# A DRAIN on GpSimd's queue behind its last adding transfer, in a hybrid Mamba-2 and latent-attention layer

## The chip, the cores and the metric

The kernel runs on one core of a Trainium2 chip. Five engines work side by side, each with its own queue of instructions: TensorE (PE) multiplies matrices, VectorE (DVE) and ScalarE (ACT) do elementwise work, GpSimd (POOL) does elementwise work and issues transfers, and SyncE (SP) only issues transfers and waits. They are kept in step by semaphores. A DRAIN is an instruction on such a queue that does no work: what stands behind it waits until the DRAIN is done. The metric is the device time of one execution in microseconds (us). The kernel before takes 643.44 us, the median of 3 runs (643.41 to 643.98).

## The reference, cut to what matters

The program computes one layer of a streaming encoder for 512 prompt tokens and 64 tokens of a running stream, together 576 columns of a transposed activation: a normalisation, a projection, a state-space branch and a latent-attention branch, an output projection, a gated feed-forward block, and a last normalisation.

```python
def hybrid_layer(x, ckv_past, krope_past, ssm_h0, conv_buf, p):
    h = rmsnorm(x, p['norm_mix'])
    proj = h @ p['w_in']
    ...
    x = x + jnp.concatenate([y_ssd, o], axis=-1) @ p['w_out']
    hf = rmsnorm(x, p['norm_ffn'])
    x = x + (jax.nn.silu(hf @ p['w_gate']) * (hf @ p['w_up'])) @ p['w_down']
    return x, c_kv, k_rope, h_new, conv_new

y_prompt = rmsnorm(xp, norm_final)
y_sample = rmsnorm(xs, norm_final)
```

What bears on this change is the end: the last part of the product with `w_down`, added to `x`, and the last `rmsnorm` over 1024 channels.

## The kernel before, in words

Activations lie with channels on the 128 partitions and the 576 tokens along the free axis, so 1024 channels are 8 tiles, numbered `t`. Each fp32 operand is split into a high and a low part, and a product is three matrix multiplications.

The feed-forward block runs over 22 tiles of `d_ff` in parts (`CUTS`). While TensorE computes gate and up for one part, it also computes `w_down` for the part before. These partial sums don't stay on the chip's memory near the engines: `acc[0]` and `acc[1]` are two arrays in DRAM. The first part is written there (`down_plain`, lines 1009 and 1012), the four next parts are added by transfers that GpSimd issues with `accum_op=ALU.add` (`send`, line 1064). After the last of them each half of `acc[0]` (four tiles) is read back by SP (line 1143) into the tile `sum_0` or `sum_1`, and the same half of `acc[1]` is added onto it by two transfers of GpSimd (line 1145), four in all. These are GpSimd's last adding transfers, and the last transfers that it issues at all.

Then comes the last part of the product (`NL` tiles of `d_ff`, weights `wd`), done for two groups of tokens, `parts`: columns 0 to 319 and 320 to 575. For each group and tile TensorE multiplies (line 988), VectorE adds the result to `sum` (line 1163), ScalarE squares it (line 1202 in the first group, 1251 in the second) and scales it (line 1167). The squares are summed over tiles in `ss3`, which lies in the tile `fz`. In the first group GpSimd adds tiles 0, 2 and 4 (line 1207, three TENSOR_TENSOR), VectorE sums the others in `sq_last` and adds them at the end (lines 1212 and 1210). TensorE sums `ss3` over channels (line 1244), and ScalarE and VectorE turn that into the factor of the normalisation. In the second group GpSimd adds seven tiles (line 1256). The outputs are multiplied by the factor on VectorE (lines 1177 and 1173), two of the second group on GpSimd (line 1175, the last two TENSOR_TENSOR), and sent out by SP and ScalarE (line 1183).

Behind this the framework puts the end of the program, which the profile shows at line 1482, where the program is finished: SP waits for every outstanding transfer; every engine runs a DRAIN; PE, DVE, ACT and SP report to a semaphore; GpSimd, after its own DRAIN, waits for the four reports and releases the four. Semaphores are then cleared and the same exchange is done once more. The start of the program (line 1479) has one such exchange too.

The order of each engine's instructions is written out by hand: the table `ISSUE` holds, for each engine, the places of its instructions in the order of their making, and `issue_in_order` ties each to the next. GpSimd's row ends with

```python
137 136 138 140 139 141-143 145 144 146-148
```

Places 144 to 148 are transfers of line 1064. The four of line 1145 (149 to 152) and the twelve TENSOR_TENSOR (153 to 164) are not in the row; they keep the order in which they are made.

Of the kernel before, what the change touches and what calls it, by code (L numbers as in the profile page):

```python
# [54 lines left out]
def hybrid_layer_kernel(ctx: ExitStack, tc: tile.TileContext, a, o):  # L55
    nc = tc.nc
    pe, act, dve, pool, sp = nc.tensor, nc.scalar, nc.vector, nc.gpsimd, nc.sync
# [1082 lines left out]
    for i2, tag in enumerate(("bc", "sz")):  # L1140
        x2t[i2] = z = midp.tile([P, 4, T], F32, tag=tag, name=f"sum_{i2}")
        rows = lambda i, n: acc[i][n].rearrange("t p c -> p t c")
        sp.dma_start(z, rows(0, slice(4 * i2, 4 * i2 + 4)))
        for j in (0, 2):
            pool.dma_start(z[:, j : j + 2], rows(1, slice(4 * i2 + j, 4 * i2 + j + 2)), accum_op=ALU.add)
        x2.extend(z[:, j] for j in range(4))

    NL = len(prev)
    wd = [weights(a["w_dlast"][i], 1024, f"dl{i}") for i in range(NL)]
# [236 lines left out]
    "POOL": """  # L1386
0-3 7 18 28 4 8 5 9 6 10 26 11 27 12 29 13-17 20-23 19 24-25 31 30 32-42 53 55 57 59 54 56 58 60 43-52 61-69 71 73 75
70 77 79 81 74 76 72 83 78 80 82 84-87 89 88 90 92 91 93-103 105 104 106 108 107 109-119 121 120 122 124 123 125-135
137 136 138 140 139 141-143 145 144 146-148
""",  # L1390
    "SP": """
11-14 16 15 17-20 23 22 25 21 24 31 26 32 39-40 36 33 38 41-42 37 43-47 55 77 62 79 54 56 58 63 81 57 60 59 61 68 66
# [102 lines left out]
```

## Time and profile before

| what | value |
|---|---|
| median of 3 runs (lowest to highest) | 643.44 us (643.41 to 643.98) |
| the profiled execution, its own time | 643.93 us |
| its span, first to last instruction | 642.2 us |
| granted TensorE clock, mean | 0.995 |
| busy: PE, DVE, ACT, POOL | 626.6, 543.0, 400.7, 110.2 us |

Each time in a view counts from the start of the span. A row of the timeline gives start, duration, engine, line, operation, the tile written and the tile read, and in brackets how long the engine had been idle and what ended that. DRAINs and semaphore instructions run on an engine's queue (POOLq, SPq and so on) and aren't counted as busy time, so they are missing from the busy rows and are seen in the view of their line.

### The profile page before, as it was taken

What the parts mean: (1) busy time and instruction counts of PE and PEld (TensorE: products, weight loads), DVE (VectorE), ACT (ScalarE), POOL (GpSimd) and SP (SyncE); (2) the same over time, 40 slices, a digit from 0 to 9 for tenths busy, and PEclk for the clock granted to TensorE, in tenths of its full rate; (3) what the DMA queues carried; (4) which work ended last, traced back from release to release, by engine and by line L of the source; (5) the groups of instructions that cost most, each with busy time, mean ns of one, the idle gap of its engine ahead of it and who ended that gap; (6) DMA issues with size and microseconds to landing.
All of it is one profiled execution on the core that took longest, in us unless ns stands there. A gap on an engine that the chain in (4) does not pass through costs nothing.

```text
span 642.2 us, 12089 instructions
## 1 busy us (share of the span) xinstructions
PE 626.6 (98%) x4635; PEld 598.8 (93%) x4635; DVE 543.0 (85%) x945; ACT 400.7 (62%) x768; POOL 110.2 (17%) x164
## 2 busy tenths in 40 slices
PE   9998999999999999999999999999999999999994
PEld 8898999986788799999999999999999999999993
DVE  6998986899876699999999879988898889976554
ACT  7644436678775567766556666566657665765463
POOL 1321103101010000001301330033103210332323
PEclk9999999999999999999999999999999999999998
DMA  9322265321231133245743985398639883789904
GB/s 317 131 61 69 85 169 158 107 80 53 94 121 61 57 109 110 76 124 179 250 134 93 229 171 146 94 184 204 140 97 179 196 181 99 140 203 274 232 2 147
DMA packets 39593, 89.19 MB, mean 139 GB/s; under 512 B 4570, under 2 KB 14312, under 8 KB 39280
## 3 DMA queue, kind: packets, MB, share of 16 engines
q1 hardware_dynamic: 26416, 63.12, 31.0%
q0 software_dynamic: 12400, 24.73, 21.0%
q8 instruction: 36, 0.59, 0.4%
q10 hardware_dynamic: 720, 0.57, 0.3%
q14 instruction: 21, 0.17, 0.1%
HBM read 62.74 MB, written 24.53 MB: 136 GB/s over the span
## 4 chain that ended last, share of the span: by engine, by line
PE 83%; DVE 3%; ACT 1%; issue 1%; DMA 1%; POOL 1%; POOLq 0%; DVEq 0%; ACTq 0%
PE ps_x L852 21%; PE ps_d L1050 14%; PE ps_z L852 10%; PE ps_o L443 8%; PE ps_y L852 5%; PE ps_in L128 4%; PE ps_z L443 3%; PE ps_l L988 3%; PE ps_d L988 2%; PE ps_p L852 2%; PE sc L657 2%; PE pv L704 1%; PE ptp L679 1%; PE ps_v L590 1%; PE ps_q L443 1%
## 5 line engine op out<-in xcount | busy, mean ns | idle before, releaser
L852 PE MATMUL ps_x<-xop,wh_gu_S 128*128 128x288 f32 x504 | 101.7, 295 | 0.0
L852 PEld LDWEIGHTS ps_x<-xop,wh_gu_S 128*128 128x128 f32 x504 | 80.7, 188 | 0.2
L852 PE MATMUL ps_x<-xop,wl_gu_S 128*128 128x288 f32 x252 | 74.0, 294 | 0.0
L113 DVE TENSOR_TENSOR wl_gu_S<-gu,wh_gu_S 128x1024 fp32r<-128x1024 f32 x44 | 53.5, 1221 | 10.5 <-ACT wh_gu_S L112 6.9
L1064 POOL DMA_DIRECT2D acc<-fz x32 | 28.0, 910 | 167.3 <-ACT fz L1061 138.5
L112 ACT CAST wh_gu_S<-gu 128x1024 fp32r<-128x1024 f32 x44 | 46.3, 1052 | 15.9 <-PE ps_y L852 8.3
L128 PE MATMUL ps_in<-xs,wh_in 128*128 128x288 f32 x256 | 45.3, 298 | 2.0 <-DVE sp_a L351 1.8
L852 PEld LDWEIGHTS ps_x<-xop,wl_gu_S 128*128 128x128 f32 x252 | 47.3, 188 | 0.0
L128 PEld LDWEIGHTS ps_in<-xs,wh_in 128*128 128x128 f32 x256 | 37.6, 189 | 3.1 <-ACT up L381 2.0
L852 PE MATMUL ps_z<-xop,gu_a 128*128 128x288 f32 x252 | 38.3, 295 | 0.0
L852 PEld LDWEIGHTS ps_z<-xop,gu_a 128*128 128x128 f32 x252 | 35.0, 188 | 0.0
L852 PE MATMUL ps_z<-xop,wh_gu_S 128*128 128x288 f32 x168 | 34.9, 297 | 0.0
L852 PE MATMUL ps_x<-xop,wh_gu_A 128*128 128x288 f32 x168 | 34.6, 297 | 0.0
L852 PE MATMUL ps_y<-xop,wh_gu_A 128*128 128x288 f32 x168 | 34.0, 294 | 0.0
L443 PE MATMUL ps_o<-cat_y,wh_out 128*128 128x288 f32 x128 | 29.3, 312 | 0.4 <-ACT cat_y L142 0.4
L112 ACT CAST wh_gu_A<-gu 128x1024 fp32r<-128x1024 f32 x22 | 23.1, 1051 | 10.4 <-PE ps_x L852 7.0
L113 DVE TENSOR_TENSOR wl_gu_A<-gu,wh_gu_A 128x1024 fp32r<-128x1024 f32 x22 | 26.8, 1220 | 1.4 <-ACT wh_gu_A L112 1.0
L852 PEld LDWEIGHTS ps_z<-xop,wh_gu_S 128*128 128x128 f32 x168 | 27.2, 189 | 0.3 <-ACT wh_gu_S L112 0.3
L128 PE MATMUL ps_in<-xs,wl_in 128*128 128x288 f32 x128 | 27.4, 296 | 0.0
L852 PEld LDWEIGHTS ps_x<-xop,wh_gu_A 128*128 128x128 f32 x168 | 27.1, 189 | 0.1
L852 PEld LDWEIGHTS ps_y<-xop,wh_gu_A 128*128 128x128 f32 x168 | 26.9, 188 | 0.0
L443 PE MATMUL ps_z<-xs,wh_z 128*128 128x288 f32 x128 | 26.4, 299 | 0.0
(384 smaller groups left out, 2011.5 us busy)
## 6 DMA issues: line engine op xcount, KB each, us to landing
gu<-in_w_gu SPq DMA_DIRECT2D x44, 512.0 KB, 5.2
wr_d<-in_w_down SPq DMA_DIRECT2D x18, 512.0 KB, 4.4
acc<-fz POOLq DMA_DIRECT2D x16, 288.0 KB, 6.3
acc<-da POOLq DMA_DIRECT2D x16, 288.0 KB, 7.8
acc<-dc POOLq DMA_DIRECT2D x16, 288.0 KB, 8.2
wr_in<-in_w_in SPq DMA_DIRECT2D x8, 512.0 KB, 4.5
wr_out<-in_w_out SPq DMA_DIRECT2D x8, 512.0 KB, 3.4
cumb<-cumD SPq DMA_DIRECT2D x5, 512.0 KB, 4.3
```

Source lines behind the costliest of these rows:

```text
L112: act.copy(hi, raw)
L113: dve.tensor_tensor(lo, raw, hi.bitcast(F32), ALU.subtract)
L128: pe.matmul(ps[:m, hf, :n], w, x[:, hf * n : (hf + 1) * n], start=start and k == 0 and i == 0, stop=stop and k == last and i == 2,)
L443: pe.matmul(ps[:, :n], w, x[:, cols], start=k == 0 and i == 0, stop=k == len(terms) - 1 and i == 2,)
L590: pe.matmul(ps[:n], l, r, start=j == 0, stop=j == 2)
L657: pe.matmul(s[:, :nk], qs[:, j, q0 : q0 + P], ks[:, j, :nk], start=True, stop=True)
L679: pe.transpose(pp[:, k : k + P], prs[p, i][:, j, b * P : b * P + P], ident)
L704: pe.matmul(pv[64 * j : 64 * j + 64, b * P :], V[b][:, h * HD : (h + 1) * HD], pts[p, b, j], start=b == 0, stop=True, skip_group_check=b > 0,)
L852: pe.matmul(ps, p, q, start=not onto and first and kp == kps[0] and j == 0, stop=onto or (last and kp == kps[-1] and j == 2), skip_group_c ...
L988: pe.matmul(ps, w, x[:, cols], start=first and k == 0 and i == 0, stop=last and k == len(terms) - 1 and i == 2,)
L1050: pe.matmul(ps, p, v, start=not onto and n == 0 and j == 0, stop=onto or (n == len(ks) - 1 and j == 2), skip_group_check=onto,)
L1064: pool.dma_start(out, src, accum_op=ALU.add)
```

## The change

One line is added behind the loop that issues the adding transfers of line 1145, and GpSimd's row in the table is made longer.

```diff
         for j in (0, 2):
             pool.dma_start(z[:, j : j + 2], rows(1, slice(4 * i2 + j, 4 * i2 + j + 2)), accum_op=ALU.add)
         x2.extend(z[:, j] for j in range(4))
+    pool.drain()
 
     NL = len(prev)
...
-137 136 138 140 139 141-143 145 144 146-148
+137 136 138 140 139 141-143 145 144 146-153
```

The new instruction is made right after the four transfers, so it has place 153 of GpSimd's instructions, and `146-153` ties it behind them (149 to 152). In the built program it stands directly behind the fourth, waits for no semaphore and raises none. The number of instructions on every other engine is unchanged, and from line 1147 on every line number is one higher.

GpSimd's rows from the last adding transfers to the end of its queue, before (-) and now (+), as the built programs have them; `sum` are the two tiles of the result, `acc` the partial sums in DRAM, `fz` holds the sums of squares, `R` the factor. A DRAIN is not among the rows that such a listing holds:

```order
 L1145 DMA sum_7378<-acc_3186 128x2x576 x2
 L1145 DMA sum_7382<-acc_3186 128x2x576 x2
-L1207 TENSOR_TENSOR fz<-fz,sq 128x320 x3
-L1256 TENSOR_TENSOR fz<-fz,sq 128x256 x7
-L1175 TENSOR_TENSOR sum_7378<-sum_7378,R_99 128x256 x2
+L1208 TENSOR_TENSOR fz<-fz,sq 128x320 x3
+L1257 TENSOR_TENSOR fz<-fz,sq 128x256 x7
+L1176 TENSOR_TENSOR sum_7378<-sum_7378,R_99 128x256 x2
```

Nothing moved against anything else: the rows differ by their line numbers alone, and the DRAIN stands between the second and the third of them.

## The prediction

> **What bounds the kernel now.** I read the page first, for the whole; then the end of the program, because the change stands 40 us before it.
>
> ```profile
> span 642.2 us, 12089 instructions
> ...
> PE 626.6 (98%) x4635; PEld 598.8 (93%) x4635; DVE 543.0 (85%) x945; ACT 400.7 (62%) x768; POOL 110.2 (17%) x164
> ...
> PE 83%; DVE 3%; ACT 1%; issue 1%; DMA 1%; POOL 1%; POOLq 0%; DVEq 0%; ACTq 0%
> ```
>
> TensorE bounds nearly all of it, and GpSimd, the engine that gets the DRAIN, is busy for 17%. Work added to GpSimd in the middle of the program has idle time to lie in. What matters is who is last at the end, so next I read the view of line 1482, which holds the end of the program (each row: engine's queue, operation, count, duration in ns as min/median/max, first and last start). First the stretch from 630 to 641 us, then from 641 us on:
>
> ```profile
> L1482 SPq EVENT_SEMAPHORE  x9: 28/28/28, 636.1 to 638.4; - x9
> L1482 SPq DRAIN  x2: 7/7/7, 638.5 to 638.5; - x2
> L1482 PEldq DRAIN  x1: 1083/1083/1083, 632.9 to 632.9; - x1
> L1482 DVEq DRAIN  x1: 2166/2166/2166, 633.6 to 633.6; - x1
> L1482 POOLq DRAIN  x1: 7051/7051/7051, 634.4 to 634.4; - x1
> L1482 ACTq DRAIN  x1: 151/151/151, 636.4 to 636.4; - x1
> ```
>
> ```profile
> L1482 POOLq EVENT_SEMAPHORE  x4: 17/17/17, 641.5 to 642.1; - x4
> L1482 POOLq DRAIN  x3: 46/93/7051, 634.4 to 642.0; - x3
> L1482 SPq EVENT_SEMAPHORE  x2: 17/17/17, 641.6 to 642.2; - x2
> ```
>
> Each engine runs a DRAIN, reports to a semaphore on which GpSimd waits, and is released by GpSimd. The reports are in at 634.0 (632.9 + 1.08, PE), 635.8 (633.6 + 2.17, DVE), 636.5 (ACT) and 638.5 (SP, which first waits for the output transfers). GpSimd's own DRAIN ends at 641.45 (634.4 + 7.05), and only then do its semaphore instructions begin, at 641.5. So between 638.5 and 641.45 the kernel waits for one instruction. SP's side says the same (waits of SP's queue: in total, times, longest):
>
> ```profile
> SPq L1482 <- PEq L1482: 3.6, 2, 3.1
> SPq L1482 <- DMA out_yT<-sum: 1.9, 6, 0.4
> ```
>
> The 3.1 us are put down to PE, which had long reported (634.0); the wait is for GpSimd. Is GpSimd working then? The chain of waits ends with its last two pieces, and the transfers from 634 to 642.2 us (40 slices of 0.205 us) show no traffic late in it:
>
> ```profile
> 634.40 0.76 POOLq L1482
> 635.16 0.68 POOL sum L1175
> ```
>
> ```profile
> GB/s 0 0 0 0 260 370 325 340 335 360 320 345 355 325 350 335 350 335 340 75 0 0 0 0 0 0 0 0 0 0 0 0 0 0 0 0 0 0 0 0
> ...
> q10 hardware_dynamic: 576, 0.52, 19.7%
> q1 hardware_dynamic: 576, 0.52, 19.5%
> ```
>
> The last multiplication ends at 635.84 (635.16 + 0.68). From there the DRAIN lasts another 5.6 us (641.45 − 635.84), 3.3 of them with no byte moving (20 slices: after 638.1), and no code is fetched (neither instruction queue has a packet in this window). The two later DRAINs in the same view took 46 and 93 ns. Thus the 5.6 us are not the price of any DRAIN; they belong to something left over since the previous one. That previous one is at the program's start:
>
> ```profile
> 0.42 0.10 POOL L1479 MEMSET const-uint8-127<- 128x1 uint8 x1
> ```
>
> ```profile
> L1479 POOLq DRAIN  x1: 188/188/188, 0.4 to 0.4; - x1
> ```
>
> It began under MEMSETs, the last of which ended at 0.52, and was over by about 0.6 (0.4 + 0.188): under 0.1 us behind its engine's last work. Plain work on GpSimd therefore leaves nothing long behind. What lies between the two and not before the first are the transfers that GpSimd issues.
>
> **The change part by part.** Nothing is removed; one DRAIN is added between the last adding transfer (L1145) and the first addition of squares (L1207). GpSimd's timeline there:
>
> ```profile
> 599.66 2.44 POOL L1145 DMA_DIRECT2D sum<-acc  x2 [2.57 <-PE ps_y L852]
> 614.84 0.88 POOL L1207 TENSOR_TENSOR fz<-fz,sq 128x320 f32<-128x320 f32 x1 [12.73 <-ACT sq L1202]
> 616.15 0.89 POOL L1207 TENSOR_TENSOR fz<-fz,sq 128x320 f32<-128x320 f32 x1 [0.43 <-ACT sq L1202]
> 617.32 0.88 POOL L1207 TENSOR_TENSOR fz<-fz,sq 128x320 f32<-128x320 f32 x1 [0.29 <-ACT sq L1202]
> ```
>
> *The new DRAIN itself.* It can start at 602.10 (599.66 + 2.44), and the instruction behind it waits for ScalarE's square until 614.84: 12.7 us of cover. Its price is bounded below by 0.1 us (the DRAIN at the start) and above by the late one's 5.6 us, counted from when the transfers have landed in case it waits for them. The transfers from 600.2 to 615 us (slices of 0.37 us) end so:
>
> ```profile
> GB/s 199 212 206 206 212 199 212 206 199 218 199 206 256 193 205 193 206 199 206 199 218 218 205 131 50 31 12 0 0 0 0 0 0 0 0 0 0 0 0 0
> ```
>
> Traffic stops after 27 slices, at 610.2. The new DRAIN then ends between 602.2 and 615.8 (610.2 + 5.6). I take about 610, its leftover worked off while the last transfer still runs. Even the upper end costs nothing: the first addition would start 1.0 us late, and three of 0.88 us back to back would end at 618.5 instead of 618.2 (617.32 + 0.88). Next in line for their result is VectorE's addition of line 1210:
>
> ```profile
> 619.93 0.49 DVE L1210 TENSOR_TENSOR fz<-fz,sq_last 128x320 f32<-128x320 f32 x1
> ```
>
> That is 1.7 us after 618.2. So the early price is 0; the cover is gone once the DRAIN ends later than 617.2 (619.93 less three of 0.88). Queued behind the DRAIN are only GpSimd's twelve additions and multiplications and the end; no transfer of its own comes after it, and SP's and ScalarE's output sends go by their own queues.
>
> *The late DRAIN.* After the change, what lies between it and the previous DRAIN is twelve TENSOR_TENSOR and no transfer. Lower bound: 0.1 us behind 635.84, as at the start. Upper bound: 5.6 us as now. A middle value, if the price went by the number of instructions since the last DRAIN: 5.6 / 164 x 12 = 0.4 us. I take the lower end, since the start's row is the only DRAIN here behind work without transfers; 0.4 would do as well, because what decides is only whether it ends before SP reports at 638.5, that is, whether it falls below 2.7 us (638.5 − 635.84).
>
> Here the trace and a rule of the notes part. The late DRAIN ended 5.6 us behind its engine's last work. The Trainium skill (PSUM — Partial Sum Buffer, Engine vs sequencer instructions) says that a drain waits for its engine to go fully idle and names nothing more; by that alone it would have been over near 635.9, so the trace differs from it, or the engine wasn't idle in a way that no busy row shows. By that rule the early DRAIN would leave the late one as it is, and the sum would be 0.
>
> *The sum.* GpSimd's report moves from 641.45 to about 635.9, SP's at 638.5 becomes the last, and everything behind it follows: 641.45 − 638.55 = 2.9 us gained. SP's row agrees: of its 3.1 us about 0.1 remains (GpSimd's signal at 641.5, SP's answer at 641.6). It can't be more than 3.1, since SP is held to 638.5 by output transfers that the change doesn't touch. The profiled execution took 643.93 us (1.73 outside its span) and would take 641.0; it stood 0.49 above the median of the three runs, 643.44, so the forecast is 643.44 − 2.9 = **640.5 us**.
>
> **The rivals.**
>
> *A: the late DRAIN costs the same again.* Its 5.6 us might be owed to something that the twelve TENSOR_TENSORs or the idle time before them bring, or to a count over the whole program. For it: no row shows a DRAIN on GpSimd behind a TENSOR_TENSOR alone; that at the start stood behind MEMSETs. Against it: the 46 and 93 ns right after, which a count over the whole program wouldn't allow. Gain 0: 643.4. The rule above comes out here. Another page would put the price down to code: the Trainium skill (GPSIMD Engine Reference, Instruction dispatch) gives about 6 us for the first call of freshly loaded code; the trace, with no instruction packet in that window, speaks against a load there.
>
> *B: slower. The early DRAIN holds the additions.* The mechanism: a DRAIN pays for each transfer still in flight, begins over when the last has landed, and pays again at the end whatever came before. With the price twice behind the landing it ends at 610.2 + 5.6 + 5.6 = 621.4, 4.2 us past the point of 617.2 from which it decides, and the late price stays. VectorE's L1210 then starts 4.2 us late, and with it the norm on TensorE:
>
> ```profile
> 620.78 0.48 DVE L1210 TENSOR_TENSOR fz<-fz,sq 128x320 f32<-128x320 f32 x1
> 621.68 0.70 PE L1244 MATMUL ps_n<-fz,ones 128*128 128x320 f32 x2
> ```
>
> The slack between the two is 0.4 us (621.68 less 621.26), so 3.8 us reach the end: 647.2. Against it: the late DRAIN ran with output transfers of other queues in flight until 638.1 and took no visible extra, and there are 12.7 us of idle time to use up first.
>
> *C: a part only.* The late DRAIN keeps between 2.7 and 5.6 us. At 4.2, half way, the gain is 1.4 us: 642.0. Nothing but a price that goes by time since the last transfer would do this.
>
> **How the numbers follow.** Forecast 0.82, A 0.10, B 0.05, C 0.03. A measurement of this kernel can tell about 0.2%, 1.3 us, from no change; 2.9 is 0.45%. The forecast and half of C are faster: 0.83; A and the other half are the same: 0.12; B is slower: 0.05. The three runs lie 0.57 us apart. Low end: the largest gain from the lowest run and that spread, 643.41 − 3.1 − 0.57 = 639.7. High end: the smallest gain that can be told, 643.44 − 1.3 = 642.1, which takes in half of C. The range leaves out A, B and the rest of C, somewhat under 2 in 10.
>
> **What would show it.** Line 1147 has a DRAIN of GpSimd that starts near 602.1 and ends before 614.8, some 8 us long if it waits for the landing. The first addition of squares still starts when ScalarE's square is done. The DRAIN of the program's end ends near 635.9, with SP's DRAIN next and last at 638.5, and SP's 3.1 us wait is gone. I am wrong if the late DRAIN still ends 5.6 us behind the last multiplication (A), or if the additions of squares start late and L1210 with them (B).

## The result, and the profile after

The changed kernel takes 640.83 us, the median of 8 runs (639.76 to 642.54); the kernel before, run beside it on the same chip, 643.61 us (8 runs, 642.94 to 643.98). The ratio is 0.996 with a 95% interval of 0.9948 to 0.9972. The whole interval lies below 1: faster, by 2.8 us or 0.4%.

The end of the program is now line 1483 and the new DRAIN line 1147. The page's first line, the view of the new DRAIN's line, and, in the view of the end's line, the rows of the DRAINs and of GpSimd's semaphore instructions, all of the changed kernel:

```profile
span 638.1 us, 12090 instructions
```

```profile
L1147 POOLq DRAIN  x1: 14736/14736/14736, 599.4 to 599.4; - x1
```

```profile
L1483 POOLq EVENT_SEMAPHORE  x4: 17/17/17, 637.3 to 638.0; - x4
L1483 POOLq DRAIN  x3: 34/93/1515, 633.2 to 637.8; - x3
L1483 SPq DRAIN  x3: 7/7/7, 637.2 to 637.5; - x3
```

The long DRAIN of the end took 7051 ns and takes 1515. The chain of waits of the changed kernel shows where in it the engine's last work ends:

```profile
633.16 0.76 POOLq L1483
633.92 0.68 POOL sum L1176
```

The last multiplication ends at 634.60 (633.92 + 0.68), the DRAIN at 634.67 (633.16 + 1.515): 0.07 us behind it, where it was 5.6. GpSimd's semaphore instructions start at 637.3, right behind SP's first DRAIN at 637.2, so SP reports last. The waits of SP's queue from 600 us on agree:

```profile
SPq L1483 <- DMA out_yT<-sum: 1.9, 6, 0.4
...
SPq L1483 <- PEq L1483: 0.6, 2, 0.5
```

The output transfers hold SP for the same 1.9 us; of the 3.6 us behind them 0.6 are left. From the end of the last multiplication to the end of the span it was 6.4 us (642.2 − 635.84) and is 3.5 (638.1 − 634.60). These 2.9 us are the change. The two profiled spans differ by 4.1 us; the other 1.2 lie ahead of the last multiplication (635.84 − 634.60), and the changed kernel's profiled execution, 639.76 us, is the fastest of its eight. The medians, 2.78 us apart, agree with the 2.9.

The early DRAIN came out otherwise than forecast. GpSimd's timeline after the last adding transfers, ScalarE's first square, and the transfers from 599.5 to 614.5 us (40 slices of 0.375 us):

```profile
598.92 2.44 POOL L1145 DMA_DIRECT2D sum<-acc  x2 [2.75 <-DVE g L964]
614.21 2.93 POOL L1208 TENSOR_TENSOR fz<-fz,sq 128x320 f32<-128x320 f32 x3 [12.85 <-ACT sq_last L1203]
```

```profile
613.04 0.47 ACT L1203 ACTIVATE sq<-sum 128x320 f32<-128x320 f32 x1 [3.72 <-DVE sum L1164]
```

```profile
GB/s 203 197 203 215 215 221 197 228 209 190 203 197 215 215 203 203 197 215 197 209 203 209 117 49 25 12 0 0 0 0 0 0 0 0 0 0 0 0 0 0
```

The record of the DRAIN opens at 599.36, while the last two issues still run (to 601.36), and ends at 614.10 (599.36 + 14.736). Traffic stops after 26 slices, at 609.25: the DRAIN waits for the landing and then takes 4.8 us more. The first square is ready at 613.51 and the first addition starts at 614.21, 0.1 behind the DRAIN. It was held 0.6 us. Before, no DRAIN stood there.

### The profile page after: what moved, and what is told of

Its sections match the earlier page's. It is cut to its first block, busy times and chain, and to the rows that moved or that the text cites. A ratio compares the mean times of both kernels' runs of the same rounds, so it can differ in the third digit from the quotient of the medians.

```text
span 638.1 us, 12090 instructions
## 1 busy us (share of the span) xinstructions
PE 627.0 (98%) x4635; PEld 598.9 (94%) x4635; DVE 543.5 (85%) x945; ACT 400.9 (63%) x768; POOL 110.4 (17%) x164
## 4 chain that ended last, share of the span: by engine, by line
PE 84%; DVE 3%; ACT 1%; issue 1%; POOL 1%; DMA 1%; POOLq 0%; DVEq 0%; ACTq 0%
PE ps_x L852 21%; PE ps_d L1050 14%; PE ps_z L852 11%; PE ps_o L443 8%; PE ps_y L852 5%; PE ps_in L128 4%; PE ps_z L443 3%; PE ps_l L988 3%; PE ps_d L988 2%; PE ps_p L852 2%; PE sc L657 2%; PE pv L704 2%; PE ptp L679 1%; PE ps_v L590 1%; PE ps_q L443 1%
```

## The experiments

What has to be told apart: does the end's DRAIN pay for transfers issued since the previous DRAIN (and how much for each), for something else that the early DRAIN clears, or a fixed price once, wherever the last DRAIN stands? Most of the kernels below were timed by one execution, which tells little of a difference this small; what the end's DRAIN costs is read in each one's trace, against the last multiplication. All kernels start from the kernel before with the same edit: GpSimd's row of the table stays as it was, and a short table of its own places each DRAIN behind one of GpSimd's instructions and ahead of the next. Places count GpSimd's instructions from 0: 69 to 84 are the first part's plain transfers (lines 1009 and 1012), 85 to 148 the adding ones of line 1064, 16 in each part, 149 to 152 those of line 1145, 153 to 164 the additions and multiplications. GpSimd issues 108 transfers in all. Lines behind the new code move: the DRAINs are line 1148, the additions 1209 and 1258, the last multiplications 1177, the end of the program 1492 (1500 in two kernels).

```diff
         x2.extend(z[:, j] for j in range(4))
+    for _ in DRAINS:
+        pool.drain()
...
+        if name == "POOL":
+            stops = [i for i in made if type(i).__name__ == "InstDrain"]
+            made = [i for i in made if type(i).__name__ != "InstDrain"]
+            for (behind, ahead), d in zip(DRAINS, stops, strict=True):
+                tc.add_manual_dep(d, made[behind].name, info, reason="drain order")
+                tc.add_manual_dep(made[ahead], d.name, info, reason="drain order")
...
+DRAINS = ((155, 156),)
```

**The DRAIN behind the three additions of the first group**, as above: no transfer of GpSimd's is in flight there, and GpSimd would be idle for 3.4 us only.

> The one DRAIN stands behind the third addition of squares (L1207 of the kernel before) instead of ahead of the first, some 8 us after the last transfer has landed. Backlog theory (a DRAIN on GpSimd pays about 52 ns, 5.6 us / 108, for each transfer that GpSimd issued since its last DRAIN): it lasts 5.6 us, from 618 to about 624 us, holds the first addition of the second group (621.6) by some 2 us, and the DRAIN at the end is short; 640.8 us. Rival, the price is waiting for transfers in flight and some 4.5 us behind their landing: here it's under 0.2 us, and the time is 640.8 too or the end's DRAIN pays 5.6 again and it is 643.6.

It took 642.65 us, the kernel before beside it 645.33. The view of the DRAIN's line, then GpSimd's timeline around it:

```profile
L1148 POOLq DRAIN  x1: 6506/6506/6506, 617.3 to 617.3; - x1
```

```profile
617.33 0.87 POOL L1209 TENSOR_TENSOR fz<-fz,sq 128x320 f32<-128x320 f32 x1 [0.29 <-ACT sq L1204]
623.91 1.69 POOL L1258 TENSOR_TENSOR fz<-fz,sq 128x256 f32<-128x256 f32 x2 [5.70 <-ACT nr_y L173]
```

The DRAIN ends at 623.81 (617.30 + 6.506), 5.61 us behind the addition that it stands behind (617.33 + 0.87): to the hundredth what the end's DRAIN took in the kernel before (641.45 − 635.84), and the end's is down to 0.07 (636.33 + 1.512 − 637.77), by the chain's last pieces and the row of its line:

```profile
636.33 0.76 POOLq L1492
637.09 0.68 POOL sum L1177
```

```profile
L1492 POOLq DRAIN  x3: 34/93/1512, 636.3 to 640.7; - x3
```

So the whole price moves with the first DRAIN behind the transfers. It needs no transfer in flight: the last had landed 7 us earlier.

**The DRAIN earlier**: ahead of the last of the four adding parts, so that 20 transfers come after it, and ahead of all four, so that 68 do.

```diff
-DRAINS = ((155, 156),)
+DRAINS = ((132, 133),)
```

> The one DRAIN stands in the 28 us gap ahead of the fourth part's adding transfers (near 520 us), so that 20 transfers follow it. Backlog theory: the end's DRAIN lasts 20 x 52 ns = 1.0 us behind the last multiplication, ends ahead of SP's report, and the gain is whole: 640.8 us. Rival, a fixed price after any transfer: 5.6 us behind the last multiplication, 643.6 us.

```diff
-DRAINS = ((155, 156),)
+DRAINS = ((84, 85),)
```

> The one DRAIN stands ahead of the first part's adding transfers (near 330 us), so that 68 transfers follow it. Backlog theory: the end's DRAIN lasts 68 x 52 ns = 3.5 us behind the last multiplication, 0.8 us past SP's report: about 641.6 us. Rival, a fixed price after any transfer: 5.6 us, 643.6 us.

They took 641.12 and 641.89 us (before: 645.33). The chain's last two pieces and the rows of the end's DRAINs, first with 20 transfers left:

```profile
634.49 0.76 POOLq L1492
635.25 0.68 POOL sum L1177
```

```profile
L1492 POOLq DRAIN  x3: 46/98/3153, 634.5 to 639.1; - x3
L1492 SPq DRAIN  x3: 7/7/7, 638.6 to 638.9; - x3
```

then with 68:

```profile
634.47 0.77 POOLq L1492
635.24 0.68 POOL sum L1177
```

```profile
L1492 POOLq DRAIN  x3: 46/98/4916, 634.5 to 639.9; - x3
L1492 SPq DRAIN  x3: 7/7/7, 638.6 to 639.6; - x3
```

Behind the last multiplication the DRAIN lasts 1.71 us with 20 (634.49 + 3.153 − 635.93) and 3.47 with 68 (634.47 + 4.916 − 635.92). A fixed price is out. With 20 it has ended 1.0 us ahead of SP's report at 638.6 (at 637.64) and costs nothing; with 68 it ends 0.8 us after it and GpSimd is last again. But 20 cost 82 ns each beyond the 0.07, and 68 only 50: one price for each of all 108 doesn't fit either.

**Both**: ahead of the last part and behind the last transfer.

```diff
-DRAINS = ((155, 156),)
+DRAINS = ((132, 133), (152, 153))
```

> Two DRAINs: that near 520 us and that of the changed kernel near 600 us, with 20 transfers between them. In the changed kernel the latter ended 4.5 to 5 us behind the landing of the last transfer. Backlog theory: it ends 0.2 to 1.0 us behind the landing, near 610.5, and holds no addition. Rival, a fixed price behind the landing: 614 again. The end's DRAIN is short by both, and the time 640.8 us.

It took 641.50 us. The second of its early DRAINs, in the view of its line from 595 us on, and the transfers from 599.5 to 614.5 us (slices of 0.375 us):

```profile
L1148 POOLq DRAIN  x1: 12069/12069/12069, 600.4 to 600.4; - x1
```

```profile
GB/s 209 203 209 215 203 160 172 209 197 209 209 203 203 247 203 203 203 197 215 203 197 203 221 215 209 203 203 190 43 12 12 0 0 0 0 0 0 0 0 0
```

It ends at 612.4, 1.2 us behind the last packet (31 slices: 611.1 to 611.2), where with 108 transfers behind the previous DRAIN it was 4.8. No addition is held. So an early DRAIN does two things in turn: it waits for the landing, and it then takes a time that goes with its count of transfers.

**Does the size count, or the number?** Sixteen transfers of one column behind the early DRAIN, on top of the 20; and a single one behind the changed kernel's DRAIN. They write to an array that nothing reads.

```diff
-DRAINS = ((155, 156),)
+DRAINS = ((132, 133),)
...
+    scr = dpool.tile([16, P, 1], F32, name="scr")
+    for i in range(16):
+        pool.dma_start(scr[i], ones[:, :1])
```

> The DRAIN near 520 us, and right behind it, in the same gap, sixteen more transfers of GpSimd, of one column each (128 x 4 bytes) into a scratch array that nobody reads. So 36 transfers follow the DRAIN, and hardly more bytes than the 20 of the run before. Price by number of transfers (0.9 us + 41 ns each, from 20 at 1.71 us and 88 and 108): the end's DRAIN lasts 2.4 us behind the last multiplication. Rival, price by bytes or rows moved: 1.7 us as with 20.

```diff
-DRAINS = ((155, 156),)
+DRAINS = ((152, 153),)
...
+    scr = dpool.tile([1, P, 1], F32, name="scr")
+    for i in range(1):
+        pool.dma_start(scr[i], ones[:, :1])
```

> The DRAIN of the changed kernel, and between it and the first addition one more transfer of one column, so that one transfer follows the DRAIN. If the price has a fixed part for any transfer since the last DRAIN, the end's DRAIN lasts 0.9 to 1.0 us behind the last multiplication; if it goes by number alone, 0.1 us. The first addition starts about 0.6 us later than in the changed kernel, and the time stays within 0.5 us of it.

The single one took 641.23 us, the sixteen 648.36 (before: 644.39). The time of the sixteen says nothing of the DRAIN: behind the first eight, GpSimd's queue, by its waits, stood still five times until small transfers had landed, so the adding transfers behind them, and with them the whole end, came late; the last multiplication ended 6.7 us later than with 20 alone (642.61 and 635.93). GpSimd's waits from 540 to 612 us:

```profile
POOL scr L1290 <- DMA scr<-ones: 11.8, 3, 5.2
...
POOL acc L1064 <- DMA scr<-ones: 7.5, 2, 6.6
```

The price at the end can still be read from the chain's last pieces and the row of the end's DRAINs. With sixteen:

```profile
641.17 0.76 POOLq L1500
641.93 0.68 POOL sum L1177
```

```profile
L1500 POOLq DRAIN  x3: 46/98/4458, 641.2 to 646.1; - x3
```

with one:

```profile
634.61 0.76 POOLq L1500
635.37 0.68 POOL sum L1177
```

```profile
L1500 POOLq DRAIN  x3: 46/93/1596, 634.6 to 639.3; - x3
```

They end 3.02 us (641.17 + 4.458 − 642.61) and 0.16 us (634.61 + 1.596 − 636.05) behind the last multiplication. One small transfer adds 0.09; sixteen add 1.31 to the 1.71, 82 ns each, the same as the large ones. In the second kernel the small transfer also stood between the DRAIN and the first addition, which started at 616.62, 1.1 us behind the DRAIN's end (615.47) where it was 0.1.

**Where in between does the rate change?** 4, 36 and 52 transfers left:

```diff
-DRAINS = ((155, 156),)
+DRAINS = ((132, 133), (148, 149))
```

> Two DRAINs, near 520 us and between the last transfer of line 1064 and the first of line 1145, so that only the four of line 1145 (two tiles each) follow. So far the end's DRAIN took, behind the last multiplication, 0.16 us after 1 small transfer, 1.71 after 20, 3.02 after 36 (16 of them small), 3.47 after 68, 5.61 after 108. If each transfer costs the same 82 ns up to some number: 4 cost 0.4 us. If the price goes by kind, 37 ns for one of line 1064 and 260 for one of line 1145: 1.1 us. The DRAIN in front holds the first two transfers of line 1145 by 2 to 5 us, which may cost the kernel up to 2 us.

```diff
-DRAINS = ((155, 156),)
+DRAINS = ((116, 117),)
```

> One DRAIN in the gap ahead of the third part's adding transfers (near 453 us), so that 36 transfers follow it, 32 of line 1064 and four of line 1145. If each costs 82 ns up to some number: the end's DRAIN takes 3.0 us behind the last multiplication, as with 20 and 16 small ones. If the price goes by kind (37 and 260 ns): 2.3 us, and the time is that of the changed kernel.

```diff
-DRAINS = ((155, 156),)
+DRAINS = ((100, 101),)
```

> One DRAIN in the gap ahead of the second part's adding transfers (near 387 us), so that 52 transfers follow it. Behind the last multiplication the end's DRAIN took 0.07 us after 0 transfers, 0.16 after 1, 0.40 after 4, 1.71 after 20 and 3.02 after 36, which is 0.07 + 0.082 for each, whatever its size; but 3.47 after 68 and 5.61 after 108, where that would give 5.65 and 8.93. If the number goes on to count at 52: 4.34 us, and the time is about 1.6 us over the changed kernel. If entries begin to be cleared between 36 and 52: less, 3.0 to 3.5 us.

They took 640.41 and 642.95 us (before: 644.27) and, on another chip, 642.74 (before: 643.59). In the first, with 4 left, GpSimd is idle for 9.98 us ahead of the first two transfers of line 1145, instead of 8.50 with the one DRAIN ahead of the last part and 7.02 in the kernel before: they are held 1.5 to 3.0 us, near the lower end of what was expected, and the time of 640.41 us does not show it. The rows of 36:

```profile
635.99 0.76 POOLq L1492
636.75 0.68 POOL sum L1177
```

```profile
L1492 POOLq DRAIN  x3: 46/98/4460, 636.0 to 641.0; - x3
```

The DRAIN ends 3.02 us behind the multiplication (635.99 + 4.460 − 637.43), as with 20 large and 16 small transfers. The rows of 52, and its SP's wait from 630 us on:

```profile
634.47 0.76 POOLq L1492
635.23 0.68 POOL sum L1177
```

```profile
L1492 POOLq DRAIN  x3: 46/97/5768, 634.5 to 640.8; - x3
L1492 SPq DRAIN  x3: 7/7/7, 638.5 to 640.5; - x3
```

```profile
SPq L1492 <- PEq L1492: 2.3, 2, 1.8
```

The DRAIN ends at 640.24, 4.33 us behind the multiplication and 1.7 behind SP, which waits 1.8: most of the gain is gone. All kernels together, with the price as the DRAIN's end less the last multiplication's end:

| transfers issued since the previous DRAIN | price, us | 0.07 + 0.082 for each |
|---|---|---|
| 0 (the changed kernel; behind the additions; both) | 0.07 | 0.07 |
| 1 (small) | 0.16 | 0.15 |
| 4 | 0.40 | 0.40 |
| 20 | 1.71 | 1.71 |
| 36 (20 large, 16 small) | 3.02 | 3.02 |
| 36 (all large) | 3.02 | 3.02 |
| 52 | 4.33 | 4.33 |
| 68 | 3.47 | 5.65 |
| 108 (before; the early DRAIN behind the additions) | 5.61 | 8.93 |

Up to 52 the price is 82 ns for each transfer, whatever its size. The rates put down ahead of these runs, which took the line to be straight up to 68 and 108 or split it by the kind of transfer, fell; the 3.5 us forecast for 68 came true at 52 ns each, a rate that 20 and 52 refute, and so by luck. Past 52 the price lies below the line: 3.47 us are by it the price of 41 transfers, and 5.61 that of 68. Whether some of them are cleared without a DRAIN, and by what, no run shows; it stays open.

The early DRAINs of the same kernels have something to say on it. They stand right behind their transfers, so their time is taken from the end of the last packet that GpSimd's transfers moved:

| transfers since the previous DRAIN | last packet ends, us | DRAIN ends, us | between, us |
|---|---|---|---|
| 16 (four left, its second) | 595.22 | 596.23 | 1.00 |
| 20 (both, its second) | 611.24 | 612.43 | 1.19 |
| 40 (68 left) | 326.78 | 328.81 | 2.03 |
| 56 (52 left) | 392.15 | 394.85 | 2.70 |
| 72 (36 left) | 460.59 | 463.94 | 3.35 |
| 88 (20 left; four more executions: 3.92 to 3.99) | 526.59 | 530.51 | 3.91 |
| 108 (the changed kernel) | 609.28 | 614.10 | 4.82 |

That is about 41 ns for each transfer, with no bend past 52. A DRAIN right behind the landing thus takes about half as much for each as one long after it, and there all of up to 108 count. Whether the rest is done while the DRAIN waits for the landing, no run tests.

**Is an earlier place better than the changed kernel's?** There the first addition isn't held. Both kernels, timed in five rounds on one chip with the kernel before:

```diff
-DRAINS = ((155, 156),)
+DRAINS = ((152, 153),)
```

> The changed kernel again (DRAIN behind the last adding transfer, tied by a table of its own), timed beside the next: 2.8 us under the kernel before, a ratio of 0.9955.

```diff
-DRAINS = ((155, 156),)
+DRAINS = ((132, 133),)
```

> The DRAIN near 520 us, with 20 transfers behind it, timed. In its profile no addition is held, and VectorE's two additions into sq_last that took 0.78 and 0.69 us in the changed kernel take 0.53. If the hold costs anything, this is faster than the changed kernel by 0.2 to 0.5 us; if not, the same: ratio 0.9955 to the kernel before.

| kernel | median us (lowest to highest) | ratio to before, 95% |
|---|---|---|
| before | 644.39 (643.25 to 646.29) | |
| the changed kernel's place | 641.15 (640.57 to 643.42) | 0.9956 (0.9938 to 0.9974) |
| ahead of the last part | 641.44 (640.01 to 642.69) | 0.9952 (0.9936 to 0.9969) |

The gain is there again, and the two places can't be told apart: both prices are below the 2.7 us that SP's report covers. No kernel tried beats the changed one by more than the measurement tells.

## Why the prediction was right, point by point

*Who is last.* Right. GpSimd's DRAIN was the last to be done, SP came next and is now last, and it is as far behind the last multiplication as it was (637.2 − 634.60 = 2.6; 638.5 − 635.84 = 2.7).

*What the 5.6 us are.* Right that they are left over from transfers that GpSimd itself issued. It was argued from the start's DRAIN and the 46 and 93 ns; the table shows it, by a price that goes with their count.

*The late DRAIN.* I took the lower end, 0.1 us, and it measured 0.07. The middle value, 0.4 us by the number of instructions, is refuted: twelve additions and multiplications behind the early DRAIN left nothing.

*The early DRAIN.* Mis-sized, on the path of nothing. "I take about 610, its leftover worked off while the last transfer still runs" and "some 8 us long" failed: it took 14.7 us and ended at 614.1, 4.8 us behind the traffic, near the upper bound of 5.6. The expectation that the first addition would start as soon as its square is ready failed with it, by 0.6 us. The step beside it, that even the upper end costs nothing, held, though the additions also got in VectorE's way. VectorE's rows around the sum of the first group, in the changed kernel:

```profile
615.62 0.78 DVE L1213 TENSOR_TENSOR sq_last<-sq_last,sq 128x320 f32<-128x320 f32 x1 [0.23 <-ACT sq L1203]
616.33 0.49 DVE L1164 TENSOR_TENSOR sum<-ps_l,sum 128x320 f32<-128x320 f32 x1
616.80 0.69 DVE L1213 TENSOR_TENSOR sq_last<-sq_last,sq 128x320 f32<-128x320 f32 x1
...
618.70 0.49 DVE L1211 TENSOR_TENSOR fz<-fz,sq_last 128x320 f32<-128x320 f32 x1
```

GpSimd's three additions end at 617.14 (614.21 + 2.93), 1.56 us ahead of the addition on VectorE that needs them; two of VectorE's own took 0.78 and 0.69 us, and ended in time too. In the kernel before the two took 0.53 each:

```profile
616.85 0.53 DVE L1212 TENSOR_TENSOR sq_last<-sq_last,sq 128x320 f32<-128x320 f32 x1 [0.23 <-ACT sq L1202]
...
618.02 0.53 DVE L1212 TENSOR_TENSOR sq_last<-sq_last,sq 128x320 f32<-128x320 f32 x1
```

*The sum.* 2.9 us forecast, 2.9 in the two traces' ends and 2.78 between the medians. The 0.1 us between these is below what the runs can tell.

*Rival A, the same cost again.* Refuted by the 0.07. The rule quoted from the Trainium skill (PSUM — Partial Sum Buffer, Engine vs sequencer instructions), that a drain waits for its engine to go fully idle, leaves out what decided here. The code load of the other page of the Trainium skill (GPSIMD Engine Reference, Instruction dispatch) doesn't fit a price that follows the count of transfers down to 0.16 us.

*Rival B, the early DRAIN holds the additions and the late price stays.* Half of its mechanism is real: the DRAIN does wait for the landing and then pays. But it pays once, and the late price goes. With the DRAIN behind the additions the held work did cost 0.9 us (below), so the risk lay in the place, not in the instruction. The point from which B reckoned is 617.3 by its own terms (619.93 less 2.64), not 617.2; that changes nothing.

*Rival C, a part only.* It did not come. A part of the gain can be lost, with 52 or 68 transfers behind the DRAIN, but by their count, not by time as C had it.

## What to carry to other kernels

Look at the end of the program for the engine that reports last, and at how far its DRAIN ends behind its last work: a long DRAIN on GpSimd with no row beside it was here the backlog of the transfers it issued, 82 ns for each up to 52. A DRAIN in a gap of GpSimd's queue works that off early; what counts is how many transfers follow it, and here some 32 (2.7 us of cover less 0.07, by 0.082) may follow at no cost. Choose a gap longer than landing and backlog together, and look at what stands right behind the DRAIN, because held work starts beside other work than before.

## What the runs showed of the hardware that was not expected

*The backlog has no row.* The price shows in no busy row, moves no byte and is put down to another engine in SP's waits; only the end of a DRAIN shows it.

*VectorE slows beside GpSimd, though not in the one addition that reads PSUM.* With the DRAIN behind the additions, the second group's first additions on GpSimd ran from 623.91 to 625.60 instead of at 621.71. VectorE's timeline there, then the same operations with the DRAIN ahead of the last part, where GpSimd is idle beside them:

```profile
623.96 1.04 DVE L177 TENSOR_TENSOR nr_u<-nr_u,nr_v 128x320 f32<-128x320 f32 x1 [0.18 <-ACT nr_u L174]
625.03 0.93 DVE L178 SCALAR_TENSOR_TENSOR ps_n<-nr_u,nr_y 128x320 f32<-128x320 f32 x1
```

```profile
624.04 0.49 DVE L177 TENSOR_TENSOR nr_u<-nr_u,nr_v 128x320 f32<-128x320 f32 x1 [0.18 <-ACT nr_u L174]
624.57 0.50 DVE L178 SCALAR_TENSOR_TENSOR ps_n<-nr_u,nr_y 128x320 f32<-128x320 f32 x1
```

The two took 1.04 and 0.93 us instead of 0.49 and 0.50, and GpSimd's later additions wait for what follows them: the last of these ends at 631.03 instead of 630.14. That is 0.9 us of the 1.84 by which this kernel's last multiplication ended later (637.77 to 635.93); the rest is the next point. In the changed kernel the additions of line 1213 took 0.78 and 0.69 us beside GpSimd, while line 1164, which reads one operand from PSUM, took 0.49 between them. The Trainium skill (SBUF — State Buffer, SBUF: two separate sides) says that a VectorE operation with two inputs from SBUF and a GpSimd operation that reads SBUF take a port pair in turns, as an exclusive lock. Which operations slow down agrees with it.

*TensorE's last small products take longer when the granted clock is halved ahead of them.* The kernel with the DRAIN ahead of the last part was profiled in two executions. Of each, the row of the eight products, then the view by stages for 633 to 634 us (after the five engines' busy times: granted clock, DMA share, GB/s):

```profile
632.88 1.16 PE L1280 MATMUL ps_r<-diag,ones 128*128 128x128 f32 x8 [0.41 <-DVE diag L1277]
```

```profile
633.00:634.00 1.00, 1.00 (x8) 0.84 (x8) 0.37 (x2) 0.00 (x0) 0.00 (x0) 1.00 0.00 0
```

```profile
632.36 1.97 PE L1280 MATMUL ps_r<-diag,ones 128*128 128x128 f32 x8 [0.41 <-DVE diag L1277]
```

```profile
633.00:634.00 1.00, 1.00 (x7) 1.00 (x5) 0.48 (x2) 0.00 (x0) 0.00 (x0) 0.50 0.00 0
```

The same eight products took 1.16 us at a clock of 1.00 and 1.97 at 0.50. Of the thirteen profiled executions ten have the 1.16, all at 1.00; the other three, which have 1.80 to 2.07, all have 0.50 from 633 to 634 us: this one, that with both DRAINs, and that with the DRAIN behind the additions. In the last of them, from GpSimd's last addition of squares to the last multiplications it took 5.30 us instead of 4.35, which is the other 0.95 of its 1.84. Why the clock was halved earlier in these three no run shows. Each profiled time above carries this spread of almost 1 us, and so the prices are read against the last multiplication, not from the times.
